# Hybrid attention block, MLP stage: sums of six tile pairs moved to later pairs, weight norms read there, deeper operand preparation in the second product, a row maximum taken earlier

## The chip, the core and the metric

The kernel runs on one core of a Trainium2 chip. The metric is device time in microseconds (us) of one execution of the whole program; lower is better. Engines: PE (matrix products), DVE (VectorE, elementwise work), ACT (ScalarE), POOL (GpSimd), and SP, whose queue issues nearly all DMAs. Each runs its own instructions in order and waits on the others by semaphores. "Pair", "step" and "operand set" below are terms of this kernel.

## What is computed

One transformer layer over 1024 tokens of width 1024, in float32. The change lies in the MLP at its end:

```python
h = rmsnorm(x, g_ff_pre[l])
y = jnp.square(jax.nn.relu(h @ w_ff1[l])) @ w_ff2[l]      # 1024x1024 @ 1024x4096, squared ReLU, @ 4096x1024
x = x + rmsnorm(y, g_ff_post[l])
```

Everything ahead of it (two attention groups, cross-attention to a memory, their projections and norms) is the same code in both kernels.

## The kernel before

Both MLP products use a Strassen-Winograd scheme on 2x2 blocks (seven block products instead of eight), and each float32 product is made of three fast matmuls on a high and a low part: `hi*hi + hi*lo + lo*hi` (lines 195 to 197). In the first product and in most of the second the parts are 16-bit, scaled by powers of two.

**Product one** runs over 16 pairs of hidden-feature blocks (j = 0 to 15). A pair makes the four quadrants of the hidden activation: `g11`, `u3` (the 12 block, later reduced by `pv`), `g22`, `u2`. Seven block products are needed per pair; for j < 7 (`AHEAD`) two of them were made earlier and are read back from DRAM (`reload`, tile `p1r`), so pairs 0 to 6 have 60 matmuls and pairs 7 to 15 have 84. On PE the order within a pair is (h3T products if j >= 7), `px` (T2), `pz` (T1), `px` again (T3, adding to the same bank), `pv` (T4), `pz` again (B22, adding to the same bank). So DVE or ACT must have read `px` before T3 starts, and DVE must have read `pz` (for `g22`) before B22 starts.

After relu and square on ACT (`relu2`, which also leaves a row sum of squares in `hsq`), the pair's quadrants are combined for the second product's Winograd sums. Closure `sums`, called one pair later, makes `s1 = u2 + g22`, `u2 = g11 - u2`, `s2 = s1 - g11`, `s4g = u3 - s2` on DVE (lines 2668 to 2674), stores each to DRAM (`put`, `put_parts`; tensors `gd` and `gi`), and after every odd pair `put_sums` makes four half-width DVE sums for each of two inner blocks and stores them (lines 2200 to 2206).

In the same pair the weights of the next pair are combined: three subtractions and additions and a fourth (lines 2387, 2388, 2389, 2394), on DVE for pairs below 7 and on POOL after that, then split into high (ACT, line 2148) and low parts (DVE, line 2151). Each pair also loads two blocks of `w_ff2` (`norm_load`, tile `w2n`) and squares them on ACT for the weight norm `w2sq` (line 1144), 32 blocks in 16 pairs.

**Product two** has 68 steps, numbered s. Steps 0 to 7 use the T1 sums with 32-bit parts, tile `fy`; later steps use 16-bit parts: 32 steps on full blocks (`fx`) with 28 half-size inner steps (`fi`) between them. For a step, `fetch` loads the left rows `ra` and the right weights (`wg` or `wi`), `combine` makes a weight sum on DVE, `prepare` makes four operand tiles (two ACT, two DVE), `multiply` runs 24 matmuls. Before, three operand sets rotate, `prepare(s + 2)` stands at the head of step s, and `fetch(s + 4)` follows. `second_scales`, at the head of step 3, computes the two scales for the 16-bit steps: PE sums the weight norms (`norms`), DVE takes the row maximum of `hsq` into `scs`, PE transposes that (`top`), DVE and POOL finish. The last three steps run once per output tile, with the final norms and stores (`finish`) between. `later` is a list of such norm work (`squares`, `inverse`, `finish`), from which each step calls one or two entries.

The order of instructions on each engine is that of the code (a manual schedule); tiles come from pools (`u4` has 30 buffers of 4 KB per partition, `wraw` 3, `t2` 18), and a tile waits until its buffer's last user is done.

Of the kernel before, what the change touches and what calls it, by code (L numbers as in the profile page):

```python
# [14 lines left out]
F32 = mybir.dt.float32  # L15
F32R = mybir.dt.float32r
# [121 lines left out]
def build(ctx, tc, nc, out, t):  # L138
# [16 lines left out]
    def u4(name, shape, dt=F32R):  # L155

        return up.tile(list(shape), dt, tag="u4", bufs=30, name=name)
# [2017 lines left out]
    def put(j, i, c):  # L2175
        nc.sync.dma_start(gd[i][j // 2][:, j % 2, :], c)
# [10 lines left out]
    def put_parts(n, j, c):  # L2187

        k, s = j // 2 % 4, j // 8
        if j % 2 == 0:  # L2190
            even[n] = c
            nc.sync.dma_start(gi[n, "A11"][s][:, k, :], c[:, :HQ])
        else:
            nc.sync.dma_start(gi[n, ("A12", "A22")][s][:, :, k, :], c.rearrange("p (a n) -> p a n", a=2))

    def put_sums(n, j, c):

        k, s, e = j // 2 % 4, j // 8, even.pop(n)
        s12, s34 = t2(f"s12_{n}{j}"), t2(f"s34_{n}{j}")
        nc.vector.tensor_add(s12[:, :HQ], e[:, HQ:], c[:, HQ:])  # L2200
        nc.vector.tensor_sub(s12[:, HQ:], s12[:, :HQ], e[:, :HQ])
        nc.vector.tensor_sub(s34[:, :HQ], e[:, :HQ], e[:, HQ:])
        nc.vector.tensor_sub(s34[:, HQ:], c[:, :HQ], s12[:, HQ:])
        return lambda: (
            nc.sync.dma_start(gi[n, ("S1", "S2")][s][:, :, k, :], s12.rearrange("p (a n) -> p a n", a=2)),
            nc.sync.dma_start(gi[n, ("S3", "S4")][s][:, :, k, :], s34.rearrange("p (a n) -> p a n", a=2)))

    def first_row(j, wa, tags=(None, None)):

        x = bank(f"px{j}", tags[0])  # L2210
        product(x, wa, 0, B11)
        yb = bank(f"py{j}", tags[1])
        product(yb, wa, HT, B21)
        p1 = t2(f"p1_{j}")
        nc.scalar.activation(p1, x, AF.Copy)
        g11 = t2(f"g11_{j}")
        return x, p1, g11, lambda: nc.vector.tensor_add(g11, yb, p1)

    was = {}

# [233 lines left out]
    def second_scales():  # L2454

        ps, pt_ = mm_tile([P, 2 * NP], "norms2", "mm"), mm_tile([P, P], "top", "mm")
        nc.tensor.matmul(ps, o1024.to_broadcast([P, P]), w2sq, start=True, stop=True)
        nc.vector.tensor_reduce(su, hsq, axis=mybir.AxisListType.X, op=ALU.max)
        nc.tensor.transpose(pt_, su.to_broadcast([P, P]), ident)
# [90 lines left out]
    def prepare(s):  # L2550

        ra = rows_a.pop(s)
        if s not in right:
            combine(s)
        rb = right.pop(s)
        half = steps[s][0] != 3
        dt = F16 if half else F32R
        if s % 3 == 1 or s == len(steps) - 1:
            ah, al, bh, bl = [u4(f"{m}{s}", (P, D), dt) for m in ("ah", "al", "bh", "bl")]
        else:  # L2560
            ah, al = [wp.tile([P, D], dt, tag=m, bufs=2, name=f"{m}f{s}") for m in ("whi", "wlo")]
            bh, bl = [pws[s % 3 // 2].tile([P, D], dt, tag=f"v{s % 3 // 2}{m}", bufs=1, name=f"v{m}f{s}")
                          for m in ("hi", "lo")]
        if half:
            nc.scalar.activation(ah, ra, AF.Copy, scale=su)  # L2565
            nc.scalar.activation(bh, rb, AF.Copy, scale=sw2)  # L2566
            nc.vector.scalar_tensor_tensor(al, ra, su, ah, op0=ALU.mult, op1=ALU.subtract)  # L2567
            nc.vector.scalar_tensor_tensor(bl, rb, sw2, bh, op0=ALU.mult, op1=ALU.subtract)  # L2568
            ops[s] = (ah, al, bh, bl)
            return  # L2570
        nc.scalar.activation(ah, ra, AF.Copy)
        nc.scalar.activation(bh, rb, AF.Copy)
        nc.vector.tensor_sub(al, ra, f(ah))
        nc.vector.tensor_sub(bl, rb, f(bh))
        ops[s] = (ah, al, bh, bl)

    with manual:
        sums, stores = (lambda: []), []
        for j in range(NP):
# [8 lines left out]
                after.load(0)  # L2588
            elif more:
                fetch(0)  # L2590
            norms = [norm_load(2 * j), norm_load(2 * j + 1)]
            for store in stores:
                store()
            if j < AHEAD:
# [3 lines left out]
                x, _, g11, add = first_row(j, w["a"])  # L2598
                add()
            if not more:  # L2600
                fetch(1)
                fetch(2)
                prepare(0)
            product(x, w["s23"], 0, XT["T2"], more=j >= AHEAD)
            u2 = t2(f"u2_{j}")
            if j < AHEAD:
                nc.vector.tensor_add(u2, x, p1)
            else:
# [14 lines left out]
            u3 = t2(f"u3_{j}")  # L2623
# [4 lines left out]
            g22 = t2(f"g22_{j}")  # L2628
            nc.vector.tensor_add(g22, z, u3)
            stores = [form() for form in forms[:1]]  # L2630
            if late:
# [3 lines left out]
            if after:  # L2635
                after.load(1)
            elif not more:
                prepare(1)
                fetch(3)
            if j + 1 < AHEAD:  # L2640
                reload(j + 1)
            for store in stores:
                store()
            v = bank(f"pv{j}")
            for norm in norms:
                norm()
            product(v, w["s1a"], HT, XT["T4"])
            if more:
                nxt.split("s1a")
# [4 lines left out]
            if more:  # L2654
                nxt.split("s4")
            relu2(u3)
            put_parts(1, j, u3)
            nc.vector.tensor_add(u2, z, u2)
            stores = [form() for form in forms[1:]]
# [4 lines left out]
            def sums(j=j, u2=u2, u3=u3, g11=g11, g22=g22):  # L2664
                if j + 1 < NP:
                    relu2(u2)
                s1, s2, s4g = t2(f"s1_{j}"), t2(f"s2_{j}"), t2(f"s4_{j}")
                nc.vector.tensor_add(s1, u2, g22)
                put(j, 3, s1)
                nc.vector.tensor_sub(u2, g11, u2)  # L2670
                put(j, 5, u2)
                nc.vector.tensor_sub(s2, s1, g11)
# [5 lines left out]
            cur, nxt = nxt, after  # L2678
        prepare(2)


# [142 lines left out]
                finished("i", x)  # L2824

        for s, (n, k) in enumerate(steps[:-3]):
            if s and s < len(steps) - 2:
                prepare(s + 2)
            for read in reads:
                read()  # L2830
            del reads[:]
# [8 lines left out]
            if s + 4 == len(steps):  # L2840
                prepare(s + 3)
# [19 lines left out]
            del later[:1 if n < 6 else 2]  # L2861
# [7 lines left out]
        assert len(later) < 4  # L2869
# [76 lines left out]
```

## Time and profile before

| | |
|---|---|
| median of 3 runs | 1459.2 us (1459.01 to 1463.08) |
| the profiled execution | 1455.45 us, of which its span 1453.7 us |
| PE busy | 97% of the span |
| DVE busy | 78% of the span |
| product one, pairs 1 to 6 | 891.28 to 979.59 us |
| product one, pairs 7 to 14 | 979.59 to 1126.34 us |
| product two | 1144.28 us to the end |

The view of windows gives, for each stretch of the span, its length, each engine's busy time, the clock that PE was granted (1.00 is full), the mean busy share of the 16 DMA engines and the rate they moved. The view of waits lists who waited for whom, with total, count and longest. Timeline rows give start, duration, engine, line and tiles, and in brackets the idle time ahead of an instruction with what ended it. Busy PE is modelled, so stalls are better read from waits and from the start times.

### The profile page before, as it was taken

How to read it: one execution, taken by the hardware profiler on the slowest of the kernel's cores; microseconds unless marked ns; L12 is line 12 of the kernel's file. 1: busy time of each engine (PE TensorE's matmuls, PEld its weight loads, DVE VectorE, ACT ScalarE, POOL GpSimd, SP SyncE). 2: the span in 40 equal slices, each digit the busy share in tenths (PEclk: the TensorE clock that was granted, in tenths of full speed). 3: DMA queues.
4: the chain of work that ended last, by engine and by line, in shares of the span. 5: the costliest groups of instructions: out<-in, count | busy, mean ns of one | idle time of the engine just before them, and what ended most of it. 6: DMA issues, size and time to landing. Idle time of an engine off the chain costs nothing. (4 is left out here: it accounts for less than half of the span.)

```text
span 1453.7 us, 22157 instructions
## 1 busy us (share of the span) xinstructions
PE 1412.0 (97%) x7510; PEld 1019.7 (70%) x7510; DVE 1140.8 (78%) x1940; ACT 964.5 (66%) x1703; POOL 370.7 (26%) x475
## 2 busy tenths in 40 slices
PE   8999999999999999999999999989999979999997
PEld 8988888888889888888888844434444665665653
DVE  6788777866677856779888787887666756899998
ACT  6567887877787835885566566677777626565653
POOL 1245455645454210311113511003332000000003
PEclk9999999999999999999999999999999989999999
DMA  7144547544535585542134638997767987686885
GB/s 277 49 129 117 178 126 254 156 159 139 156 97 152 164 297 196 189 159 88 44 133 172 224 125 284 315 321 263 236 235 250 340 288 252 230 308 231 308 290 206
DMA packets 118801, 295.70 MB, mean 203 GB/s; under 512 B 13448, under 2 KB 31888, under 8 KB 118688
## 3 DMA queue, kind: packets, MB, share of 16 engines
q1 hardware_dynamic: 118544, 294.03, 59.6%
q8 instruction: 59, 0.97, 0.3%
q14 instruction: 54, 0.44, 0.1%
q10 hardware_dynamic: 144, 0.26, 0.1%
HBM read 220.26 MB, written 65.59 MB: 197 GB/s over the span
## 5 line engine op out<-in xcount | busy, mean ns | idle before, releaser
L731 DVE TENSOR_TENSOR phl<-ptr,phl 128x512 fp32r<-128x512 f32 (+1 forms) x152 | 93.3, 616 | 37.7 <-ACT phl L734 36.8
L734 ACT ACTIVATE phl<-ptr 128x512 fp32r<-128x512 f32 (+1 forms) x152 | 81.1, 539 | 35.4 <-PE ptr L725 33.3
L768 PE MATMUL pv<-phl,vs 128*128 128x512 f32 (+1 forms) x304 | 86.4, 367 | 1.8 <-DVE phl L731 1.8
L2565 ACT ACTIVATE whif<-ra,scs 128x1024 f16<-128x1024 f32 x40 | 45.7, 1144 | 41.2 <-PE fx L196 19.7
L2711 POOL TENSOR_SCALAR rf<-sf 128x1 f32<-128x1 f32 x7 | 6.3, 894 | 258.8 <-ACT jf L2690 258.7
L2567 DVE SCALAR_TENSOR_TENSOR wlof<-ra,scs,whif 128x1024 f16<-128x1024 f32 x40 | 51.2, 1281 | 22.6 <-ACT whif L2565 22.6
L196 PE MATMUL fx<-vlof,whif 128*128 128x512 f16 x168 | 63.7, 379 | 1.8 <-DVE vlof L2568 1.8
L195 PE MATMUL fx<-vhif,whif 128*128 128x512 f16 x168 | 63.7, 379 | 0.4 <-ACT vhif L2566 0.4
L197 PE MATMUL fx<-vhif,wlof 128*128 128x512 f16 x168 | 63.7, 379 | 0.0
L768 PEld LDWEIGHTS pv<-phl,vs 128*128 128x128 f32 x304 | 55.0, 188 | 11.6 <-DVE phl L731 2.3
L782 POOL TENSOR_TENSOR o<-o 64x256 f32<-64x256 f32 x64 | 47.5, 742 | 56.8 <-DVE o L780 39.6
L2387 POOL TENSOR_TENSOR sc<-wf,wf 128x512 f32<-128x512 f32 x8 | 12.0, 1506 | 179.9 <-DMA gi1S<-s 96.7
L1606 POOL TENSOR_SCALAR mp<-mp,mst 128x256 f32<-128x256 f32 x32 | 24.6, 774 | 125.1 <-DVE mst L1605 85.8
L195 PE MATMUL k<-hT_hi,whik 128*128 128x512 f32 x128 | 53.2, 415 | 0.0
L195 PE MATMUL q<-hT_hi,whiq 128*128 128x512 f32 x128 | 52.6, 411 | 0.0
L780 DVE TENSOR_TENSOR o<-pv,o 64x512 f32<-64x512 f32 x64 | 43.9, 686 | 10.1 <-ACT o L785 9.1
L195 PE MATMUL yw<-whiwo,yT_hi 128*128 128x512 f32 x128 | 50.7, 396 | 0.0
L197 PE MATMUL q<-hT_hi,wloq 128*128 128x512 f32 x128 | 50.3, 393 | 0.0
L197 PE MATMUL k<-hT_hi,wlok 128*128 128x512 f32 x128 | 50.2, 393 | 0.0
L196 PE MATMUL k<-hT_lo,whik 128*128 128x512 f32 x128 | 50.2, 392 | 0.0
L196 PE MATMUL q<-hT_lo,whiq 128*128 128x512 f32 x128 | 50.1, 392 | 0.0
L196 PE MATMUL yw<-wlowo,yT_hi 128*128 128x512 f32 x128 | 50.1, 392 | 0.0
(818 smaller groups left out, 5129.7 us busy)
## 6 DMA issues: line engine op xcount, KB each, us to landing
wg<-in_w_ff SPq DMA_DIRECT2D x48, 512.0 KB, 5.0
ra<-gd SPq DMA_DIRECT2D x40, 512.0 KB, 4.7
wf<-in_w_ff SPq DMA_DIRECT2D x38, 512.0 KB, 4.2
wn<-in_w_ff SPq DMA_DIRECT2D x32, 512.0 KB, 4.4
w2n<-in_w_ff SPq DMA_DIRECT2D x32, 512.0 KB, 5.8
wi<-in_w_ff2q SPq DMA_DIRECT2D x28, 512.0 KB, 5.1
gd<-s SPq DMA_DIRECT2D x32, 256.0 KB, 3.2
gd<-g SPq DMA_DIRECT2D x25, 256.0 KB, 2.7
```

The lines of the kernel that those rows point to most:

```text
L195: nc.tensor.matmul(ps, lh, rh, start=start, stop=False, skip_group_check=more)
L196: nc.tensor.matmul(ps, lh, rl, start=False, stop=False, skip_group_check=more)
L197: nc.tensor.matmul(ps, ll, rh, start=False, stop=stop, skip_group_check=more)
L731: flow.put("V", at, 0.7, lambda: nc.vector.tensor_sub(pl[:, live, :], tr[:, live, :], f(ph[:, live, :])), done)
L734: flow.put("S", flow.end, 0.6, lambda ph=ph, tr=tr, live=live: nc.scalar.activation(ph[:, live, :], tr[:, live, :], AF.Copy), split)
L768: nc.tensor.matmul(pv[:, :, qs_, :], v, hl[:, :, hs, :], start=c == 0 and turn == 0, stop=last)
L780: flow.put("V", at, 0.7, lambda: nc.vector.tensor_add(o2[own], pv[own, :, :, ::step], o2[own]), lambda end: (free["pv"].give(end), flow.pu ...
L782: free["pv"].give(end), flow.put("G", end, 0.8, lambda: nc.gpsimd.tensor_add(o2[own, 0], o2[own, 0], o2[own, 1]), store)))
L1606: mul = lambda st=st, pr=pr: nc.gpsimd.tensor_scalar(pr, pr, st[:, 2:3], 1.0, op0=ALU.mult, op1=ALU.mult)
L2387: eng.tensor_sub(sc[:, k1], r0[:, k0], r1[:, k0])
L2565: nc.scalar.activation(ah, ra, AF.Copy, scale=su)
L2567: nc.vector.scalar_tensor_tensor(al, ra, su, ah, op0=ALU.mult, op1=ALU.subtract)
```

## The change

It has four parts.

- **Sums put off.** For j < 6, three of the four sums (`u2 = g11 - u2`, `s2`, `s4g`) with their stores, and both `put_sums` of the odd pairs, go into a list, `later_sums`: 6 parts and 6 `put_sums`. Pairs from 7 on call one entry (even j) or two (odd j) at their end; by pair 14 the list is empty. `s2` is now `g22 - u2` of the new `u2`. `u2` and `g22` of these pairs lie in a `u4` tile (`ug`) and `u3` takes the place of `p1` in `p1r`, so that they survive.
- **Weight norms.** Pairs 7 to 14 load four `w2n` blocks each, two squared ahead of the `pv` product and two after `relu2(u3)`; the other pairs load none.
- **Product two.** Four operand sets; steps 0 to 4 still prepare two steps ahead, step 5 prepares 7 and 8, and from there it is three ahead. Steps 0 and 1 are fetched in pair 14, 2 to 5 in pair 15, and then `fetch(s + 5)`. `ra` of the first eight steps lies in `u4`. One entry of `later` is called per step, three at the last.
- **Row maximum.** The reduction of `hsq` stands in step 1, and `second_scales` in step 4.

```diff
+    PUT_OFF = 6
+    later_sums = []
+
+    def put_off_sums(j, u2, u3, g11, g22):
+        r = {}
+        def part():
+            nc.vector.tensor_sub(u2, g11, u2)
+            put(j, 5, u2)
+            s2, s4g = t2(f"s2_{j}"), t2(f"s4_{j}")
+            nc.vector.tensor_sub(s2, g22, u2)
+            put(j, 4, s2)
+            nc.vector.tensor_sub(s4g, u3, s2)
+            put_parts(5, j, s4g)
+            r["s4"] = s4g
+        later_sums.append(part)
+        if j % 2:
+            later_sums.append(lambda: put_sums(1, j, u3)())
+            later_sums.append(lambda: put_sums(5, j, r["s4"])())
...
-        nc.vector.tensor_reduce(su, hsq, axis=mybir.AxisListType.X, op=ALU.max)
         nc.tensor.transpose(pt_, su.to_broadcast([P, P]), ident)
...
-        ra = wp.tile([P, D], F32, tag="wraw", bufs=3, name=f"ra{s}")
+        ra = (u4(f"ra{s}", (P, D), F32) if n == 3 else
+              wp.tile([P, D], F32, tag="wraw", bufs=3, name=f"ra{s}"))
...
-            norms = [norm_load(2 * j), norm_load(2 * j + 1)]
+            norms = [norm_load(4 * (j - AHEAD) + x) for x in range(4)] if AHEAD <= j < AHEAD + NK else []
...
+            put_off = j < PUT_OFF
+            both = u4(f"ug{j}", (P, 2, HT), F32) if put_off else None
+            u2 = both[:, 0, :] if put_off else t2(f"u2_{j}")
...
-            for norm in norms:
+            for norm in norms[:2]:
                 norm()
...
             relu2(u3)
+            for norm in norms[2:]:
+                norm()
...
                 nc.vector.tensor_add(s1, u2, g22)
                 put(j, 3, s1)
+                if j < PUT_OFF:
+                    put_off_sums(j, u2, u3, g11, g22)
+                    return []
...
+            if j >= AHEAD:
+                for call in later_sums[:1 + j % 2]:
+                    call()
+                del later_sums[:1 + j % 2]
...
         for s, (n, k) in enumerate(steps[:-3]):
-            if s and s < len(steps) - 2:
+            if s and s < len(steps) - 2 and s < 5:
                 prepare(s + 2)
+            if s == 5:
+                prepare(7)
+            if 5 <= s:
+                prepare(s + 3)
...
-            if s == 3:
+            if s == 1:
+                nc.vector.tensor_reduce(su, hsq, axis=mybir.AxisListType.X, op=ALU.max)
+            if s == 4:
                 second_scales()
...
-            if s + 4 < len(steps):
-                fetch(s + 4)
+            if s and s + 5 < len(steps):
+                fetch(s + 5)
...
-            for call in later[:1 if n < 6 else 2]:
+            m = 3 if s + 4 == len(steps) else 1
+            for call in later[:m]:
                 call()
```

Every engine has as many instructions after the change as before; they stand in another order. Three places show it. On DVE, in pair 4 from the sum that frees `px` to the one that frees `pz` (`u2_4` from `px4`, then `g22_4` from `pz4`), before:

```order
L2607 TENSOR_TENSOR u2_4_10731<-px4_10718,p1r4_10667 128x512
L2668 TENSOR_TENSOR s1_3_10735<-u2_3_10608,g22_3_10657 128x512
L2670 TENSOR_TENSOR u2_3_10608<-p1r3_10534,u2_3_10608 128x512
L2672 TENSOR_TENSOR s2_3_10736<-s1_3_10735,p1r3_10534 128x512
L2674 TENSOR_TENSOR s4_3_10737<-u3_3_10655,s2_3_10736 128x512
L2387 TENSOR_TENSOR sc5_10762<-wf5_10587,wf21_10665 128x512
L2388 TENSOR_TENSOR wf21_10665<-wf21_10665 128x512
L2389 TENSOR_TENSOR sc5_10762<-wf21_10665,wf5_10587 128x512
L2625 TENSOR_TENSOR u3_4_10778<-px4_10718,p1r4_10667 128x512
```

and after the change (`ug4` holds `u2` and `g22`, `p1r4` takes `u3`):

```order
L2632 TENSOR_TENSOR ug4_10655<-px4_10642,p1r4_10597 128x512
L2696 TENSOR_TENSOR s1_3_10659<-ug3_10548 128x512
L2408 TENSOR_TENSOR sc5_10678<-wf5_10533,wf21_10595 128x512
L2409 TENSOR_TENSOR wf21_10595<-wf21_10595 128x512
L2410 TENSOR_TENSOR sc5_10678<-wf21_10595,wf5_10533 128x512
L2650 TENSOR_TENSOR p1r4_10597<-px4_10642,p1r4_10597 128x512
L2654 TENSOR_TENSOR ug4_10655<-pz4_10665,p1r4_10597 128x512
L2415 TENSOR_TENSOR sd5_10696<-wf5_10533,sc5_10678 128x512
```

Three sums of pair 3 have left the stretch, and four half-width `put_sums` no longer stand between `g22` and `sd`.

On DVE, at the end of pair 10 and the start of pair 11 (`s12_59`, `s34_59` are the `put_sums` of pair 9, `g11_11` the first sum of pair 11, `s1_10` the first sum of pair 10), before:

```order
L2658 TENSOR_TENSOR u2_10_11647<-pz10_11665,u2_10_11647 128x512
L2200 TENSOR_TENSOR s12_59_11755<-s4_8_11499,s4_9_11653 128x256
L2201 TENSOR_TENSOR s12_59_11755<-s12_59_11755,s4_8_11499 128x256
L2202 TENSOR_TENSOR s34_59_11756<-s4_8_11499 128x256
L2203 TENSOR_TENSOR s34_59_11756<-s4_9_11653,s12_59_11755 128x256
L2217 TENSOR_TENSOR g11_11_11803<-py11_11788,p1_11_11801 128x512
L2668 TENSOR_TENSOR s1_10_11821<-u2_10_11647,g22_10_11700 128x512
```

and after the change:

```order
L2686 TENSOR_TENSOR u2_10_11559<-pz10_11577,u2_10_11559 128x512
L2200 TENSOR_TENSOR s12_59_11669<-s4_8_11391,s4_9_11567 128x256
L2201 TENSOR_TENSOR s12_59_11669<-s12_59_11669,s4_8_11391 128x256
L2202 TENSOR_TENSOR s34_59_11670<-s4_8_11391 128x256
L2203 TENSOR_TENSOR s34_59_11670<-s4_9_11567,s12_59_11669 128x256
L2226 TENSOR_TENSOR ug3_10548<-p1r3_10490,ug3_10548 128x512
L2229 TENSOR_TENSOR s2_3_11677<-ug3_10548 128x512
L2231 TENSOR_TENSOR s4_3_11678<-p1r3_10490,s2_3_11677 128x512
L2217 TENSOR_TENSOR g11_11_11729<-py11_11714,p1_11_11727 128x512
L2696 TENSOR_TENSOR s1_10_11747<-u2_10_11559,g22_10_11612 128x512
```

The three sums of pair 3 (`ug3`, `s2_3`, `s4_3`) stand between `put_sums` and `g11_11`, where nothing stood before.

On PE, around `top` in product two, before:

```order
L197 MATMUL fy33_12599<-vhif2_12582,wlof2_12581 128x512
L2457 MATMUL norms2_12738<-w2sq_10215,o1024_81 128x32
L2459 MATMUL top_12739<-ident_72,scs_10216 128x128
L195 MATMUL fy30_12596<-vhif3_12627,whif3_12625 128x512
L196 MATMUL fy30_12596<-vlof3_12628,whif3_12625 128x512
```

and after:

```order
L197 MATMUL fy33_12593<-bh3_12621,al3_12620 128x512
L2478 MATMUL norms2_12770<-w2sq_10215,o1024_81 128x32
L2479 MATMUL top_12771<-ident_72,scs_10216 128x128
L195 MATMUL fy30_12590<-vhif4_12672,whif4_12670 128x512
L196 MATMUL fy30_12590<-vlof4_12673,whif4_12670 128x512
```

`top` stands one step later, ahead of step 4. On DVE the reduction that it waits for stood behind the operands of step 5 and the last `put_sums`, before:

```order
L2539 TENSOR_TENSOR wg1_5_1_12646<-wg1_5_1_12646,wg0_5_1_12648 128x1024
L2573 TENSOR_TENSOR wlof5_12723<-ra5_12644,whif5_12722 128x1024
L2574 TENSOR_TENSOR vlof5_12725<-wg1_5_1_12646,vhif5_12724 128x1024
L2200 TENSOR_TENSOR s12_115_12730<-u3_14_12350,u3_15_12523 128x256
L2201 TENSOR_TENSOR s12_115_12730<-s12_115_12730,u3_14_12350 128x256
L2202 TENSOR_TENSOR s34_115_12731<-u3_14_12350 128x256
L2203 TENSOR_TENSOR s34_115_12731<-u3_15_12523,s12_115_12730 128x256
L2458 TENSOR_REDUCE scs_10216<-hsq_10214 128x1
L2460 TENSOR_REDUCE scs_10216<-norms2_12738 128x1
```

and after the change it stands ahead of the operands of step 4:

```order
L2704 TENSOR_TENSOR s2_15_12630<-s1_15_12627,g11_15_12441 128x512
L2706 TENSOR_TENSOR s4_15_12631<-u3_15_12519,s2_15_12630 128x512
L2878 TENSOR_REDUCE scs_10216<-hsq_10214 128x1
L2560 TENSOR_TENSOR wg1_4_2_12534<-wg1_4_2_12534,wg0_4_2_12536 128x1024
L2595 TENSOR_TENSOR wlof4_12671<-ra4_12532,whif4_12670 128x1024
L2596 TENSOR_TENSOR vlof4_12673<-wg1_4_2_12534,vhif4_12672 128x1024
```

The reduction moved ahead of the operands of steps 4 and 5 and of both `put_sums` of pair 15.

More of the change, by code (lines that the diff above doesn't have):

```diff
@@ L2190, in put_parts @@
         if j % 2 == 0:
-            even[n] = c
+            even[n, j // 2] = c
             nc.sync.dma_start(gi[n, "A11"][s][:, k, :], c[:, :HQ])
@@ L2196, in put_sums @@
     def put_sums(n, j, c):
-        k, s, e = j // 2 % 4, j // 8, even.pop(n)
+        k, s, e = j // 2 % 4, j // 8, even.pop((n, j // 2))
         s12, s34 = t2(f"s12_{n}{j}"), t2(f"s34_{n}{j}")
@@ L2555, in prepare @@
         rb = right.pop(s)
[L2556 to L2564, printed above, removed]
+        if steps[s][0] != 3:
+            q, x = divmod(s % 4, 2)
+            both = [pws[x].tile([P, 2, D], F16, tag=f"v{x}{m}", bufs=1, name=f"v{m}f{s}") for m in ("hi", "lo")] if q else \
+                [wp.tile([P, 2, D], F16, tag=m, bufs=2, name=f"{m}f{s}") for m in ("whi", "wlo")]
+            ah, al, bh, bl = ops[s] = [both[i][:, j] for i in range(2) for j in range(2)]
             nc.scalar.activation(ah, ra, AF.Copy, scale=su)
@@ L2568, in prepare @@
             nc.vector.scalar_tensor_tensor(bl, rb, sw2, bh, op0=ALU.mult, op1=ALU.subtract)
-            ops[s] = (ah, al, bh, bl)
             return
+        if s % 2:
+            ah, al, bh, bl = [u4(f"{m}{s}", (P, D)) for m in ("ah", "al", "bh", "bl")]
+        else:
+            ah, al = [wp.tile([P, D], F32R, tag=m, bufs=2, name=f"{m}f{s}") for m in ("whi", "wlo")]
+            bh, bl = [pws[s % 4 // 2].tile([P, D], F32R, tag=f"v{s % 4 // 2}{m}", bufs=1, name=f"v{m}f{s}")
+                          for m in ("hi", "lo")]
         nc.scalar.activation(ah, ra, AF.Copy)
@@ L2627, in build @@
                 nc.scalar.activation(u3, x, AF.Copy)
-            g22 = t2(f"g22_{j}")
+            g22 = both[:, 1, :] if put_off else t2(f"g22_{j}")
             nc.vector.tensor_add(g22, z, u3)
@@ L2656, in build @@
             relu2(u3)
+            for norm in norms[2:]:
+                norm()
             put_parts(1, j, u3)
@@ L2676, in sums @@
                 return [lambda: put_sums(1, j, u3), lambda: put_sums(5, j, s4g)] if j % 2 else []
+            if j >= AHEAD:
+                for call in later_sums[:1 + j % 2]:
+                    call()
+                del later_sums[:1 + j % 2]
             cur, nxt = nxt, after
+        assert not later_sums
         prepare(2)
@@ L2858, in build @@
             multiply(banks, range(4), [s], n in (2, 4, 6))
-            for call in later[:1 if n < 6 else 2]:
+            m = 3 if s + 4 == len(steps) else 1
+            for call in later[:m]:
                 call()
-            del later[:1 if n < 6 else 2]
+            del later[:m]
             if n == 6 and k in (3, 4):
@@ L2868, in build @@
                 finished(n)
-        assert len(later) < 4
+        assert len(later) <= 4
         last = inverse_last(7)
```

15 lines of the change are left out of this document (7 added, 8 removed).

## The prediction

> **What bounds the kernel now.** I read the view of PE's waits from pair 1 on first, then the windows by stage, then the DVE timeline at each place where PE waits.
>
> ```profile
> PE top L2459 <- DVE scs L2458: 10.5, 1, 10.5
> PE pz L195 <- DVE g L2629: 5.4, 6, 1.9
> PE px L195 <- DVE u L2607: 2.9, 4, 1.0
> PE fx L196 <- DVE vlof L2568: 1.8, 2, 0.9
> PE fx L195 <- ACT bh L2566: 1.1, 1, 1.1
> PE fx L196 <- DVE bl L2568: 0.9, 1, 0.9
> ```
> ```profile
> 891.28:979.59 88.31, 79.80 (x361) 35.01 (x360) 77.06 (x117) 64.29 (x117) 0.00 (x0) 1.00 0.90 307
> 979.59:1126.34 146.75, 146.32 (x673) 65.73 (x672) 102.06 (x131) 104.18 (x188) 45.03 (x32) 1.00 0.72 245
> 997.94:1016.28 18.34, 18.29 (x85) 8.22 (x84) 11.26 (x17) 12.90 (x24) 5.37 (x4) 1.00 0.64 226
> 1144.28:1160.99 16.71, 16.71 (x74) 13.70 (x73) 12.91 (x15) 10.69 (x17) 0.00 (x0) 1.00 0.98 354
> 1160.99:1201.45 40.46, 29.93 (x124) 24.22 (x123) 23.04 (x38) 12.55 (x15) 0.55 (x1) 0.87 0.83 287
> ```
>
> PE is the bound almost everywhere, so time can only come from its stalls, and they lie in three places: pairs 1 to 6 (first window), `top` in step 3 of product two (fifth), and the 16-bit steps late in product two (the three `fx` rows, 3.8 us). Pairs 7 to 14 (second window) have next to none. A change that moves DVE work is worth what it takes from PE in the first place, less what it puts on PE in the second.
>
> **Sums put off, pairs 1 to 6.** Pair 4 on DVE, and the PE instruction that waits for it:
>
> ```profile
> 939.19 0.69 DVE L2607 TENSOR_TENSOR u<-px,p1r 128x512 f32<-128x512 f32 x1 [1.04 <-DMA p1r<-p1d]
> ...
> 941.85 0.69 DVE L2674 TENSOR_TENSOR s<-u,s 128x512 f32<-128x512 f32 x1
> ...
> 945.23 0.69 DVE L2629 TENSOR_TENSOR g<-pz,u 128x512 f32<-128x512 f32 x1
> 945.84 0.41 DVE L2200 TENSOR_TENSOR s<-u,u 128x256 f32<-128x256 f32 x1
> ```
> ```profile
> 945.97 0.38 PE L195 MATMUL pz<-B_hi,u0hi_s 128*128 128x512 f16 x1 [0.69 <-DVE g L2629]
> ```
>
> From `u2` to `g22` DVE works without a pause, so the three sums that leave (lines 2670 to 2674, 3 x 0.69 = 2.07 us) bring `g22` forward by that much, more than the longest of the six waits for it (1.9). `u2` itself waits for `p1r`. Its load is issued behind a weight load which waits for `sd`, and `sd` follows `g22` and, every second pair, four `put_sums` of 0.41; all of that comes 2.07 to 3.7 us sooner, against waits of at most 1.0 by the PE row. The queue also loses two norm loads of 512 KB and some 0.6 MB of stores a pair from a window that is 0.90 full. ACT loses two squares. What is late next is PE alone: 84 matmuls take 18.34 us in the third window, so 60 take 13.1, six pairs 78.6, against 88.31. Gain 9.7 us, between 8.3 (the two PE rows) and 10.7 (if even the last 0.2 us a pair goes).
>
> **The same work in pairs 7 to 14.** DVE gets 6 x 2.07 + 24 x 0.42 = 22.5 us, 2.8 a pair, ahead of `g11`. The end of pair 10 and what follows, on DVE and POOL, and the PE instruction behind:
>
> ```profile
> 1056.12 1.37 DVE L2201 TENSOR_TENSOR s<-s,s 128x256 f32<-128x256 f32 x1
> 1057.41 1.48 DVE L2202 TENSOR_TENSOR s<-s 128x256 f32<-128x256 f32 x1
> 1058.82 0.41 DVE L2203 TENSOR_TENSOR s<-s,s 128x256 f32<-128x256 f32 x1
> ...
> 1062.93 0.69 DVE L2668 TENSOR_TENSOR s<-u,g 128x512 f32<-128x512 f32 x1 [3.10 <-ACT u L2173]
> ...
> 1067.99 0.68 DVE L2629 TENSOR_TENSOR g<-pz,u 128x512 f32<-128x512 f32 x1
> ```
> ```profile
> 1052.51 1.61 POOL L2387 TENSOR_TENSOR sc<-wf,wf 128x512 f32<-128x512 f32 x1 [12.42 <-DMA wf<-in_w_ff]
> ...
> 1057.29 1.33 POOL L2394 TENSOR_TENSOR sd<-wf,sc 128x512 f32<-128x512 f32 x1
> ```
> ```profile
> 1068.72 0.38 PE L195 MATMUL pz<-B_hi,u1hi_s 128*128 128x512 f16 x1
> ```
>
> `g22` ends at 1068.67 and PE takes `pz` at 1068.72: this chain has no slack from `s1` (1062.93) on, but 3.10 us of idle DVE stand before it. In such a pair the deferred part (2.07) runs after POOL's last operation (1058.62) and fits with 1.0 us left. Pairs without `put_sums` here have their time too (3.3 us for the last three rows of them) and take 3.4 to 4.1 us. Under POOL a half-width sum takes up to 1.48 instead of 0.42, so the bounds are 0, if the idle time covers all, and 24 x 1.06 + 18 x 1.06 + 22.5 = 67 us of DVE, less 8 x 3.1 idle, so 42, if every one of the 42 deferred operations is slowed like the worst row. I take 1.2, near the lower end, since POOL works 6.1 of 18.3 us in a pair and the first three slots there are already held by `put_sums` in every second pair.
>
> [...]
>
> ACT has two more squares a pair behind `relu2(u3)`, where it is idle until `px` is done; SP issues two more loads and about three more stores a pair, none ahead of a weight that is due. Bytes are the nearer question:
>
> ```profile
> w2n<-in_w_ff SPq DMA_DIRECT2D x16, 512.0 KB, 5.4
> wf<-in_w_ff SPq DMA_DIRECT2D x15, 512.0 KB, 3.9
> gd<-s SPq DMA_DIRECT2D x16, 256.0 KB, 2.9
> ```
> ```profile
> DMA packets 3355, 8.98 MB, mean 374 GB/s; under 512 B 366, under 2 KB 754, under 8 KB 3353
> ```
>
> The second window takes in 16 norm loads (8.4 MB), the put-off stores (7.4 MB, of 128 to 256 KB) and step 1's loads (1.6 MB): 17.4 MB over 146.75 us, 119 GB/s on top of 245, so 364. The last row is of 1136 to 1160 us, where the queues ran full at 374. So it fits by 3%, and transfers will land later than now.
>
> **Row maximum and `top`.** DVE ahead of the reduction:
>
> ```profile
> 1166.52 1.23 DVE L2539 TENSOR_TENSOR wg<-wg,wg 128x1024 f32<-128x1024 f32 x1 [2.61 <-DMA wg<-in_w_ff]
> ...
> 1171.56 0.21 DVE L2458 TENSOR_REDUCE scs<-hsq 128x1 f32<-128x64 f32 x1
> ```
>
> PE waits 10.5 us for this 0.21 us reduction because step 5's operands, which need step 5's loads, stand ahead of it. In step 1 it needs `relu2` alone, done long before, so `top` in step 4 waits for nothing. The clock of that window, 0.87, comes with the idle time; steps 0 to 2 took 16.71 us, so five take 27.8, against 40.46. Gain 12.6 us, the wait and the slow matmuls behind it; 10.5 if the clock drops anyway.
>
> That holds if steps 3 to 7 then find their operands. DVE has 3.67 us a step (3 x 1.22), and from step 3's operands (done 1156.0 by the same order) to step 7's there are 14.7 of operands, 2.8 of sums, 3.4 of `put_sums` and some 3 of scales: 1180, against step 7's start at 1144.3 + 7 x 5.57 = 1183. ACT needs 2.1 us a step. Loads: steps 2 to 5 are issued in pair 15, and 12.6 MB for all eight steps at 374 GB/s are 34 us, which now begin in pair 14. So nothing is short, by 3 us.
>
> **Four sets, three steps ahead.** The late waits are all for operands of a step just prepared; at the end two steps are prepared in one:
>
> ```profile
> 1432.62 1.28 DVE L2568 SCALAR_TENSOR_TENSOR bl<-wg,scs,bh 128x1024 f16<-128x1024 f32 x1
> 1433.82 4.06 DVE L2735 SCALAR_TENSOR_TENSOR xf<-yc,rf,xf 128x512 f32<-128x512 f32 x6
> ```
>
> DVE is full there, so work is not saved, only done earlier: one more step of lead is 2.6 to 3.8 us (two operations of 1.28 and mostly a combine of 1.22), and four entries of `later` (three of 0.7, one of 1.4) move behind the last operands. That is more than the waits. Gain 3.8 us of waits and about 1.1 of slow clock after them, so 4.9, between 2 (lead not reached) and 6. The moved entries add one `finish` and three `squares` (3.5 us) to a tail in which PE works 15 us; that hides them.
>
> **Sum.** -9.7 + 1.2 - 12.6 - 4.9 = -26.0 us. The profiled execution took 1455.45 us, 0.26% under the median of the runs, so 1429.4 on its footing and 1459.2 - 26.0 = 1433 on the median's, which I predict. A difference of 0.3% is about what a measurement here can tell.
>
> **Rivals.** (1) *Pairs 7 to 14 take much of it back* (0.13). A `wf` load landing later than its 3.9 us starts POOL later, and the deferred sums, which have 1.0 us to spare, run under POOL or behind it, with PE one for one behind. `w2n` at 5.4 shows loads that queue. If `wf` lands 3 us later, six pairs lose 2 us each: 1445. For it: 364 against 374 GB/s. Against: 1067.99 to 1068.72 shows no loss in any pair now. [...]
>
> (2) *The wait at `top` only moves* (0.07). If steps 5 to 7 lack their loads (2.61 us of such a wait stands above), half of the 12.6 returns: 1439. Against: step 5 is now fetched in pair 15.
>
> (3) *Slower* (0.03). [...]
>
> (4) *No change* (0.02): pairs 1 to 6 might be held by DMA (0.90 full) rather than by DVE, `top` by loads, and both waits stay under other names. Against: DVE shows no pause from `u2` to `g22`.
>
> **Numbers.** My forecast, 1425 to 1441, has 0.75. The low end is every stall gone (10.7 + 12.6 + 6) on the profiled footing, 1426, so 1424; the high end takes in rivals 1 and 2, 1446. Faster 0.95, same 0.02, slower 0.03.
>
> **What would show it.** Right: no waits of `pz` on `g` or of `px` on `u` in pairs 1 to 6, these near 79 us; no wait of `top`, and a clock near 1.00 through steps 3 to 7; pairs 7 to 14 at 18.3 to 18.6 us each; no wait over 0.5 us in the last three steps. Wrong: a wait of `pz` on `g` in pairs 8 to 13 with POOL starting more than 1 us into the pair; ACT waiting for `w2n`; DVE waiting for `wg` in steps 4 to 7; or the late `fx` waits unchanged because DVE, not its lead, is what is short.

## The result, and the profile after

The changed kernel takes 1445.95 us (median of 4 runs, 1444.89 to 1447.34), the kernel before 1459.11 (4 runs, 1457.05 to 1463.08): ratio 0.9907, 95% interval 0.9885 to 0.993. It is 13 us faster. 1433 was forecast, and a gain of 26. The time lies above the 1425 to 1441 that had 0.75, and just below 1446, the end that was set for rivals 1 and 2.

Both kernels issue 7510 matmuls, so a stage can be cut at the same matmul in both. The view of windows before (length, then busy time and instructions of PE, PEld, DVE, ACT and POOL, then clock, DMA share, GB/s), for pairs 1 to 6 from the `pz` product of pair 0 on, for pairs 7 to 15, for the steps around step 55 and for the last steps:

```profile
880.05:979.59 99.54, 90.10 (x408) 39.60 (x407) 83.04 (x124) 68.67 (x122) 5.40 (x4) 1.00 0.90 311
979.59:1144.28 164.69, 164.26 (x757) 73.89 (x756) 116.46 (x150) 115.94 (x207) 45.03 (x32) 1.00 0.74 255
1330.21:1350.01 19.80, 18.13 (x110) 10.58 (x109) 19.57 (x22) 10.46 (x10) 0.00 (x0) 1.00 0.56 199
1425.03:1440.21 15.18, 11.86 (x53) 5.08 (x52) 14.99 (x19) 4.89 (x7) 3.41 (x5) 1.00 0.61 201
```

The same matmuls after the change, with steps 3 to 7 as the third row (40.46 us before):

```profile
880.20:968.11 87.91, 87.91 (x408) 39.84 (x407) 64.75 (x88) 54.82 (x97) 5.52 (x4) 1.00 0.61 201
968.11:1152.79 184.68, 168.36 (x757) 74.59 (x756) 135.70 (x186) 131.93 (x236) 44.32 (x32) 0.97 0.87 307
1169.52:1197.23 27.71, 27.71 (x124) 22.64 (x123) 23.06 (x37) 12.60 (x14) 0.55 (x1) 1.00 0.92 346
1325.99:1344.57 18.58, 17.81 (x110) 10.59 (x109) 18.34 (x19) 10.20 (x10) 0.00 (x0) 1.00 0.59 214
1419.59:1430.82 11.23, 11.23 (x54) 5.10 (x53) 10.73 (x16) 4.48 (x11) 7.03 (x10) 1.00 0.42 157
```

| stage | forecast | measured |
|---|---|---|
| pairs 1 to 6 | -9.7 | 87.91 - 99.54 = -11.6 |
| pairs 7 to 15 | +1.2 | 184.68 - 164.69 = +20.0 |
| steps 3 to 7 | -12.6 | 27.71 - 40.46 = -12.8 |
| late product two | -4.9 | (18.58 - 19.80) + (11.23 - 15.18) = -5.2 |
| sum | -26.0 | -9.6 |

Three terms came as forecast and a little better; one missed by 19 us. The forecast's own windows are narrower than two of these. Its pairs 1 to 6 went from 88.31 to 77.70 us, so 10.6 of the 11.6; the other 1.0 is the end of pair 0. Its pairs 7 to 14 went from 146.75 to 159.06, so +12.3; the other 7.7 us are pair 15 (17.94 before, 25.62 after), for which the forecast had no term. (The two spans differ by 1453.7 - 1444.3 = 9.4, the medians by 13.2: the profiled execution before is 3.7 us under its median. Pairs 1 to 6 of the old code are one place that varies: below, two other runs with the same code there take 100.80 and 102.55 us against 99.54.)

All that PE waits for from 880 us on, after the change (total, times, longest):

```profile
PE px L195 <- ACT p L2215: 13.6, 5, 5.9
PE pz L195 <- DVE g L2654: 2.3, 2, 1.2
PE fx L195 <- DVE yc L2800: 0.8, 1, 0.8
```

The waits of pairs 1 to 6 and of `top` are gone. A new one of 13.6 us in all stands in front of T2 in five of the pairs 9 to 15: there PE adds to `px` only once ACT has copied it into `p`. With 2.3 us for `pz` and 168.36 - 164.26 = 4.1 us of slower matmuls that makes the 20.0. The longest case is pair 15, on ACT and then PE:

```profile
1128.91 1.06 ACT L1144 ACTIVATE w2n<-w2n 128x1024 f32<-128x1024 f32 x1 [7.26 <-DMA w2n<-in_w_ff]
...
1137.79 0.57 ACT L2215 ACTIVATE p<-px 128x512 f32<-128x512 f32 x1
```
```profile
1138.42 0.59 PE L195 MATMUL px<-T_hi,v1hi_s 128*128 128x512 f16 x1 [5.90 <-ACT p L2215]
1138.80 0.63 PE L196 MATMUL px<-T_lo,v1hi_s 128*128 128x512 f16 x1
```

ACT stands 7.26 us in front of a norm square of pair 14 whose load has not landed; `p` of pair 15 is queued behind it. Why the load is late is seen on SP's queue, at the turn of pair 10 to 11, before and then after:

```profile
1055.12 0.33 SPq L2192 DMA_DIRECT2D gi1A<-u  x1
1055.54 0.38 SPq L2136 DMA_DIRECT2D wf<-in_w_ff  x1
1055.97 0.92 SPq L2451 DMA_DIRECT2D w2n<-in_w_ff  x2
```
```profile
1048.55 0.33 SPq L2192 DMA_DIRECT2D gi1A<-u  x1
1052.52 0.32 SPq L2176 DMA_DIRECT2D gd<-ug  x1
1054.19 0.32 SPq L2176 DMA_DIRECT2D gd<-s  x1
1055.87 0.53 SPq L2194 DMA_DIRECT2D gi5A<-s  x1
1056.45 0.60 SPq L2136 DMA_DIRECT2D wf<-in_w_ff  x1
1057.10 1.95 SPq L2472 DMA_DIRECT2D w2n<-in_w_ff  x4
```

From the store of the old pair's `u3` (`gi1A`) to the norm loads it was 0.85 us and is now 8.55. Between them stand three stores of put-off sums, and each waits for its DVE sum:

```profile
1050.75 1.75 DVE L2226 TENSOR_TENSOR ug<-p1r,ug 128x512 f32<-128x512 f32 x1
1052.53 1.64 DVE L2229 TENSOR_TENSOR s<-ug 128x512 f32<-128x512 f32 x1
1054.20 1.64 DVE L2231 TENSOR_TENSOR s<-p1r,s 128x512 f32<-128x512 f32 x1
```

### The profile page after: what moved, and what is told of

Read it like the earlier page. It is cut to its first block, busy times and chain, and to the rows that moved or that the text cites. A ratio compares the mean times of both kernels' runs of the same rounds, so it can differ in the third digit from the quotient of the medians.

```text
span 1444.3 us, 22129 instructions
## 1 busy us (share of the span) xinstructions
PE 1409.6 (98%) x7510; PEld 1017.7 (70%) x7510; DVE 1140.6 (79%) x1940; ACT 965.3 (67%) x1703; POOL 369.8 (26%) x475
## 4 chain that ended last, share of the span: by engine, by line
PE 80%; DVE 8%; ACT 4%; DMA 4%; issue 3%; SPq 0%; DVEq 0%; ACTq 0%
PE pv L768 4%; PE ptr L725 4%; PE fx L195 3%; PE fx L197 3%; PE fx L196 3%; DMA w2n<-in_w_ff 2%; PE yw L195 2%; PE k L195 2%; PE q L195 2%; PE yw L197 2%; PE yw L196 2%; PE q L197 2%; PE k L197 2%; PE k L196 2%; PE q L196 2%
## 5 line engine op out<-in xcount | busy, mean ns | idle before, releaser
L734 ACT ACTIVATE phl<-ptr 128x512 fp32r<-128x512 f32 (+1 forms) x152 | 81.1, 540 | 35.0 <-PE ptr L725 32.9
L768 PEld LDWEIGHTS pv<-phl,vs 128*128 128x128 f32 x304 | 54.9, 188 | 11.6 <-DVE phl L731 2.3
L197 PE MATMUL yw<-whiwo,yT_lo 128*128 128x512 f32 x128 | 50.1, 391 | 0.0
L195 PE MATMUL fx<-vlof,vhif 128*128 128x512 f16 x128 | 48.5, 379 | 0.8 <-DVE yc L2800 0.8
L195 PE MATMUL fx<-wlof,whif 128*128 128x512 f16 x128 | 48.5, 379 | 0.0
L196 PE MATMUL fx<-wlof,whif 128*128 128x512 f16 x128 | 48.5, 379 | 0.0
L197 PE MATMUL fx<-wlof,whif 128*128 128x512 f16 x128 | 48.5, 379 | 0.0
```

The lines of the kernel that those rows point to most:

```text
L195: nc.tensor.matmul(ps, lh, rh, start=start, stop=False, skip_group_check=more)
L196: nc.tensor.matmul(ps, lh, rl, start=False, stop=False, skip_group_check=more)
L197: nc.tensor.matmul(ps, ll, rh, start=False, stop=stop, skip_group_check=more)
L734: flow.put("S", flow.end, 0.6, lambda ph=ph, tr=tr, live=live: nc.scalar.activation(ph[:, live, :], tr[:, live, :], AF.Copy), split)
L768: nc.tensor.matmul(pv[:, :, qs_, :], v, hl[:, :, hs, :], start=c == 0 and turn == 0, stop=last)
```

## The experiments

Theory A: the put-off stores stand ahead of the next pair's loads on SP's queue and hold them back (8.55 us at that turn instead of 0.85), the norm loads come late to ACT, and PE waits for what is queued behind them on ACT. Its rivals are B (bytes), C (four squares a pair are too much for ACT) and DVE's sums getting slower beside POOL (0.69 became 1.64 to 1.75 us at that turn). "Pairs 7 to 15" is 164.7 us before and 184.7 after.

### Stores behind the loads

```diff
-            put(j, 5, u2)
...
+            return lambda: (put(j, 5, u2), put(j, 4, s2), put_parts(5, j, s4g))
...
-                for call in later_sums[:1 + j % 2]:
-                    call()
+                stores += [call() for call in later_sums[:1 + j % 2]]
```

> The changed kernel, but the stores of the put-off sums are issued behind the next pair's loads; the DVE work stays where the change put it. Pairs 7 to 15 (first px of pair 7 to first fy) took 164.7 us before and 184.7 us after the change. Theory A (SP's queue: the weight and norm loads stand behind stores that wait for put-off DVE sums, so they are issued some 7 us late): wf is issued 2 to 4 us into a pair again, the wait of px for ACT's p (13.6 us) goes, pairs 7 to 15 take 165 to 167 us, the whole 1426 to 1430. Theory B (bytes: 364 GB/s are too much for that window): loads still land late, pairs 7 to 15 stay above 175, the whole above 1436. Theory C (four squares a pair on ACT, two of them ahead of p, are too many): no change of the 13.6 us.

1431.77 us (4 runs, 1431.08 to 1432.94), ratio to before 0.9819 (0.9792 to 0.9846). Windows, then PE's waits in pairs 7 to 15:

```profile
968.14:1137.82 169.68, 164.43 (x758) 73.91 (x756) 149.05 (x186) 131.40 (x236) 45.49 (x32) 1.00 0.94 330
```
```profile
PE px L195 <- ACT p L2215: 2.7, 1, 2.7
PE pz L195 <- DVE g L2652: 2.3, 5, 0.7
```

No DVE work was moved, only the place of stores on SP, and 15.0 of the 20.0 us went: A. The stage is nearly 3 us above A's 165 to 167. The wait that is left is pair 15's: in pair 14 the four norm loads stand behind `fetch(0)` and `fetch(1)`. Bytes are no less (330 GB/s, DMA 0.94), so B falls as the main cause.

### Norm loads ahead, weights still behind

```diff
-            norms = [norm_load(4 * (j - AHEAD) + x) for x in range(4)] if AHEAD <= j < AHEAD + NK else []
+            norms = ([norm_load(x) for x in range(4)] if j == AHEAD else next_norms) if AHEAD <= j < AHEAD + NK else []
...
+            if AHEAD <= j < AHEAD + NK - 1:
+                next_norms = [norm_load(4 * (j + 1 - AHEAD) + x) for x in range(4)]
             if j >= AHEAD:
                 for call in later_sums[:1 + j % 2]:
```

> The changed kernel, with the four norm loads of a pair issued ahead of the put-off sums of the pair before it; wf stays behind their stores. It tells the two halves of theory A apart. If ACT's wait for late norm loads is what PE sees, the wait of px for p goes and pairs 7 to 15 take 166 to 170 us (the rest are the pz waits, 2.3 us, and the slow sums beside POOL). [...]

1429.2 us (one run). Windows, then PE's waits in pairs 7 to 15:

```profile
968.67:1135.61 166.94, 164.27 (x758) 73.91 (x756) 149.31 (x186) 131.34 (x236) 44.87 (x32) 1.00 0.94 328
```
```profile
PE pz L195 <- DVE g L2654: 2.5, 5, 0.7
```

The wait of `px` for `p` is gone though stores and `wf` loads stand as after the change. So ACT's wait for late norm loads is the half that PE sees. The other half, late `wf` loads and with them slower DVE sums, is not: DVE is busy 149.31 us here against 135.70 after the change, with 186 instructions in both, and the stage is 17.7 us shorter. In pairs 7 to 15 DVE's busy time is 32.9 over before. The prediction counted 22.5 for the work itself, so an estimate of 10.4 is left for slower sums; PE's whole loss in the stage is 2.2 us.

### Norms two a pair again

```diff
-            norms = [norm_load(4 * (j - AHEAD) + x) for x in range(4)] if AHEAD <= j < AHEAD + NK else []
+            norms = [norm_load(2 * j), norm_load(2 * j + 1)]
```

> The changed kernel, but with the norm loads and squares two a pair in all 16 pairs, ahead of pv. Theory A: the two norm loads of pairs 8 to 15 are still issued 10 us into a pair and land at about 16, 2 us after ACT wants them at 14; so ACT waits 2 to 4 us in several pairs, and pairs 7 to 15 take 172 to 182 us. Theory C: px no longer waits for p, pairs 7 to 15 take under 168. Both: pairs 1 to 6 give back at most 1 of the 11.5 us, since DVE and not DMA held them.

1458.52 us (one run). Pairs 1 to 6, then 7 to 15, and what ACT waits for in the latter:

```profile
879.62:972.33 92.71, 88.83 (x409) 39.63 (x408) 64.87 (x86) 67.76 (x119) 5.40 (x4) 1.00 0.80 266
972.33:1164.83 192.50, 173.65 (x757) 75.89 (x756) 147.83 (x187) 118.99 (x210) 45.18 (x32) 0.95 0.72 251
```
```profile
ACT w2n L1144 <- DMA w2n<-in_w_ff: 25.9, 11, 9.7
```

With half the squares and 251 GB/s the stage got longer, beyond what A expected (172 to 182). ACT waits for norm loads for 25.9 us, after the change for 15.9, and PE waits for DVE's `g22` for 10.3 us instead of 2.3. Why two loads a pair are worse than four stays open: the first square of a pair stands in the same place in both. C falls, and B with it. The second expectation failed: pairs 1 to 6 gave back 4.8 us, not 1.

### Only the norms moved

The kernel before, with the change's norm lines alone:

```diff
-            norms = [norm_load(2 * j), norm_load(2 * j + 1)]
+            norms = [norm_load(4 * (j - AHEAD) + x) for x in range(4)] if AHEAD <= j < AHEAD + NK else []
...
-            for norm in norms:
+            for norm in norms[:2]:
                 norm()
...
             relu2(u3)
+            for norm in norms[2:]:
+                norm()
```

> The kernel before, with only the norm loads and squares moved (four a pair in pairs 7 to 14). Theory A: no put-off stores, so loads are issued 3 to 6 us into a pair as before; no wait of ACT for w2n over 1 us, pairs 7 to 15 take 164.7 to 166 us, the whole 1455 to 1459. Theory C: px waits for p in most pairs, pairs 7 to 15 above 172. Theory B: between, up to 168.

1447.03 us (one run). Pairs 1 to 6, then 7 to 15:

```profile
879.62:971.11 91.49, 88.71 (x409) 39.73 (x407) 81.38 (x124) 54.94 (x97) 5.68 (x4) 1.00 0.75 258
971.11:1135.80 164.69, 164.26 (x757) 73.69 (x756) 116.81 (x150) 130.21 (x236) 43.86 (x32) 1.00 0.87 303
```

Four squares a pair cost pairs 7 to 15 nothing: C is out. The stage moved 303 GB/s, nearly the 307 of the changed kernel, and lost nothing by it: B is out too. But the whole was 8 us below what I expected, all of it in pairs 1 to 6. Moving the norms alone gives 8.1 of their 11.6 us, the sums alone 6.8 (the experiment ahead of this one), both together 11.6.

### What the norms cost in pairs 1 to 6

Two edits of the kernel before: the two squares of pairs 0 to 6 behind `relu2(u3)`, and, apart from that, the squares of these pairs over 64 of 1024 columns.

```diff
-            for norm in norms:
-                norm()
+            if j >= AHEAD:
+                for norm in norms:
+                    norm()
...
             relu2(u3)
+            if j < AHEAD:
+                for norm in norms:
+                    norm()
```

> The kernel before, with only the two norm squares of pairs 1 to 6 on ACT moved behind relu2(u3); the loads stay. Moving loads and squares out of these pairs together took 8.0 us from pairs 1 to 6 (from the pz product of pair 0 to the first px of pair 7: 99.5 to 91.5 us). If the squares' place on ACT ahead of the split of s1a, for which DVE waits up to 2.5 us, is the cause: 5 to 8 us go here too. If the loads are (p1r behind w2n in SP's queue, or bytes): under 2 us go.

```diff
-        return lambda: squares_of(w, w2sq[:, n:n + 1])
+        return lambda: squares_of(w[:, :64] if n < 2 * AHEAD else w, w2sq[:, n:n + 1])
```

> The kernel before, with the norm squares of pairs 0 to 6 taken over 64 of 1024 columns (the rest of those norms is left out); the loads stay whole and in place. From the pz product of pair 0 to the first px of pair 7 the kernel before took 99.5 us, and 100.8 and 102.6 with the same code there in two other runs; without loads and squares 91.5. If it was ACT's time for the squares (2 x 1.24 us a pair): 90.5 to 94. If it was the loads (bytes, SP's queue, ACT waiting for them): 97 to 103.

1460.7 and 1455.96 us (one run each). Pairs 1 to 6 of both:

```profile
880.36:983.41 103.05, 92.59 (x409) 40.31 (x408) 83.89 (x125) 67.48 (x121) 5.40 (x4) 0.97 0.87 301
```
```profile
878.42:979.12 100.70, 90.03 (x409) 39.59 (x408) 81.89 (x124) 59.38 (x125) 5.32 (x4) 1.00 0.89 307
```

Neither the squares' place on ACT nor their time is it by itself (with the short squares ACT is busy 59.38 instead of 68.67 us, and nothing is gained). What is left are the loads. Whether by their bytes (share 0.89, and 0.75 without them), by their slots on SP or by ACT's waiting for them stays open; the last is the least likely, since with the squares moved no such wait of ACT is listed in these pairs.

### The row maximum alone

The kernel before, with one line moved out of `second_scales`, which stays in step 3:

```diff
-        nc.vector.tensor_reduce(su, hsq, axis=mybir.AxisListType.X, op=ALU.max)
...
+            if s == 1:
+                nc.vector.tensor_reduce(su, hsq, axis=mybir.AxisListType.X, op=ALU.max)
             if s == 3:
                 second_scales()
```

> The kernel before, with only the row maximum of hsq taken in step 1 instead of in second_scales, which stays in step 3. If the reduction's place in DVE's order is the whole of the wait: the wait of top (10.5 us) goes, the granted clock stays near 1.00, the five steps from fy's first matmul of step 3 on lose 12.6 us, the whole 1445 to 1448. If the later operands were short as well (rival 2 of the prediction): half of it stays as waits of fy in steps 5 to 7. If the clock falls for another reason: 10.5 instead of 12.6.

1448.83 us (one run). Steps 3 to 7, then the last steps:

```profile
1163.58:1192.12 28.54, 28.25 (x124) 22.47 (x122) 21.80 (x37) 12.53 (x15) 0.55 (x1) 1.00 0.98 354
1415.69:1433.59 17.90, 14.80 (x54) 5.70 (x53) 15.04 (x19) 4.89 (x7) 2.76 (x5) 0.81 0.66 219
```

40.46 - 28.54 = 11.9 us came from this one moved instruction, with the clock at 1.00; of the later operands one was waited for, for 0.3 us. The run's other stages gave some of it back, so the whole is just above the 1445 to 1448 expected: its last steps wait about as long as before (3.0 us against 3.3), but the clock was lower, 0.81 against 1.00, and they took 17.90 us against 15.18.

### Late product two

The change there has a lead of three steps, four operand sets with an earlier fetch, and `later` dealt out otherwise. First the changed kernel with the lead of two again:

```diff
-            if s and s < len(steps) - 2 and s < 5:
+            if s and s < len(steps) - 2:
                 prepare(s + 2)
-            if s == 5:
-                prepare(7)
-            if 5 <= s:
-                prepare(s + 3)
+            if s + 4 == len(steps):
+                prepare(s + 3)
```

> The changed kernel, with operands prepared two steps ahead throughout and steps 66 and 67 prepared together, as before; the four operand sets, the loads and the entries of later stay as after the change. If the lead is what removed the late waits of fx: they return, 3 to 5.2 us between step 55 and the end, the whole 1449 to 1451 against 1446. If it was the entries of later (one a step instead of two, three at the end): under 1 us of waits there.

1440.16 us (one run). Around step 55, and the last steps:

```profile
1320.90:1338.67 17.77, 17.77 (x110) 10.67 (x109) 17.61 (x20) 9.45 (x9) 0.00 (x0) 1.00 0.52 182
1413.69:1424.91 11.22, 11.22 (x53) 5.10 (x52) 11.20 (x15) 5.41 (x12) 6.64 (x8) 1.00 0.31 117
```

No wait is left: the lead was not it. (The whole is 5.8 us under the changed kernel's 1445.95; 3.8 of that lie in pairs 7 to 15, which the edit does not touch. That stage varies with the same code: 184.7 us after the change, 180.9 here, 184.1 in the second of the next two runs.) So the two other parts, apart: the kernel before with `later` alone, and the kernel just shown with `later` as before.

```diff
-            for call in later[:1 if n < 6 else 2]:
+            m = 3 if s + 4 == len(steps) else 1
+            for call in later[:m]:
                 call()
...
```

> The kernel before, with only the entries of later dealt as after the change: one a step, three at the fourth step from the end, instead of two in most steps. From step 55 to the end the kernel before loses 5.2 us to waits of fx that the changed kernel does not have. If the entries of later are their cause, they go here: the whole 1450 to 1452 on the footing of 1455.5. If the third operand set was (an operand tile free only when the step before has ended), they stay within 1 us.

> The changed kernel with operands prepared two steps ahead, steps 66 and 67 together, and the entries of later dealt as before (two in most steps); of the changes to product two from step 5 on only the four operand sets and the earlier fetch stay. If the fourth set is what removed the waits of fx, none over 0.5 us come back from step 55 on. If the entries of later are, 3 to 5 us come back. The waits in pairs 7 to 15 stay, since nothing is changed there.

1456.02 and 1446.45 us (one run each). `later` alone, then sets and fetch alone:

```profile
1333.92:1353.72 19.80, 18.14 (x111) 10.59 (x109) 19.57 (x22) 10.46 (x10) 0.00 (x0) 1.00 0.55 198
1428.74:1440.78 12.04, 11.38 (x54) 5.08 (x53) 11.94 (x15) 6.58 (x13) 6.39 (x7) 1.00 0.35 136
```
```profile
1324.43:1342.20 17.77, 17.77 (x111) 10.67 (x110) 17.61 (x20) 9.43 (x9) 0.00 (x0) 1.00 0.52 186
1417.21:1431.21 14.00, 11.71 (x53) 5.08 (x52) 13.87 (x17) 4.89 (x7) 2.38 (x4) 1.00 0.68 219
```

Each does its own part: sets and fetch take all of step 55's 2.0 us and 1.2 of the end's, `later` nothing of step 55's and 3.1 of the end's. Neither expectation was right as a whole. How the sets may work is in ACT's waits from 1250 us on, before, and then after the change:

```profile
ACT whif L2565 <- PE fx L196: 13.1, 7, 2.8
```
```profile
ACT vhif L2582 <- PE fx L197: 6.9, 5, 1.8
ACT whif L2582 <- PE fx L197: 6.2, 4, 2.3
```

With three sets ACT, preparing two steps ahead, waits for PE to finish with the set; in the two kernels with four sets and a lead of two no such wait is listed. With four sets and a lead of three they come back, and step 55 takes 18.58 instead of 17.77. The fourth set was not tried without the earlier fetch, so which of the two did it is not shown.

### Both orders, and the sums dealt out evenly

The changed kernel with the first two edits together; and that with the put-off sums cut into 30 pieces, dealt out by their time over pairs 7 to 14:

```diff
             if j >= AHEAD:
-                for call in later_sums[:1 + j % 2]:
-                    call()
-                del later_sums[:1 + j % 2]
+                due += 6.75
+                while later_sums and later_sums[0][0] <= due:
+                    cost, call = later_sums.pop(0)
+                    due -= cost
+                    stores.append(call())
```

> The changed kernel with two edits: norm loads ahead of the put-off sums, and stores of put-off sums behind the next pair's loads; the put-off sums come in entries as after the change. Theory A: pairs 7 to 15 take 166.5 to 167.5 us, the whole 1426 to 1429; what is left over 164.7 are the waits of pz for g22 in the pairs whose entries are longer than DVE's idle time.

> The changed kernel with three edits: norm loads ahead of the put-off sums, stores of put-off sums behind the next pair's loads, and the put-off sums cut into 30 pieces dealt out evenly, 2.8 us of DVE a pair over pairs 7 to 14. Theory A: pairs 7 to 15 take 165 to 166 us, since no pair's share is over the 3.1 us that DVE was idle; the whole 1425 to 1428. If the slow sums beside POOL matter more than their number, 167 or more.

1429.24 us (4 runs, 1427.97 to 1431.16), ratio 0.9802 (0.9783 to 0.982); and 1427.73 us (5 runs, 1426.98 to 1428.44), ratio 0.979 (0.9773 to 0.9808). Pairs 7 to 15:

```profile
968.59:1134.71 166.12, 164.26 (x757) 73.80 (x756) 143.88 (x186) 131.01 (x236) 46.16 (x32) 1.00 0.94 333
```
```profile
968.61:1134.44 165.83, 164.27 (x758) 73.81 (x756) 142.50 (x186) 131.06 (x236) 46.18 (x32) 1.00 0.94 334
```

Both are faster than the kernel before and than the changed one; between the two the difference is not clear (0.3 us in the stage). The even one came as expected; the other was 0.4 us under its range in the stage and 0.2 us over it in the whole. The even one is at 165.83 against 164.69 before: the work that pairs 1 to 6 gave away then costs 1.1 us.

## Why the prediction was right and where it was wrong

**Pairs 7 to 15, the step that failed.** The prediction said of SP that it issues "two more loads and about three more stores a pair, none ahead of a weight that is due". The stores stand ahead of the next pair's `wf` and `w2n`, and every one waits for a DVE sum. I had counted the put-off part as DVE work and as bytes, and had not followed it down SP's queue. What the step would have shown with the loads in place is in the last experiments: +1.1 us, or +2.2 with the change's own entries and only the norm loads ahead, against the +1.2 taken. So the DVE estimate held. Pair 15, 7.7 of the 20.0 us, was in no term of the sum.

**Rival 1** gave 1445 and a late landing of loads, and 1446 was measured; yet its mechanism was another, so that the time came out inside the range is luck. It had bytes make the loads late (364 against 374 GB/s): the stage moved 307, and 328 to 334 in the four kernels that lost 1 to 5 us there. And it had PE wait for DVE's `g22`: that is 2.3 of 20.0 us. "ACT waiting for `w2n`" stood among the signs of a wrong forecast, without a price. Nor was the stage's mean of 307 the most that was moved there: single slices of it, 4.6 us each, moved up to 412 GB/s.

**Sums beside POOL.** The price of up to 1.06 us for a sum beside POOL is what is seen after the change, at the turn of pair 10 to 11: 0.69 became 1.64 to 1.75, beside POOL operations of 1.30 to 1.60. What makes them slow no run here shows. In the kernel with the norm loads ahead the price comes to an estimated 10.4 us of DVE time in the stage, while PE's whole loss there was 2.2 us, so rival 3, slower, was rightly small.

**Pairs 1 to 6.** The size was nearly right (9.7 against 10.6 in the forecast's own window), the reason half of it. I put all on DVE's three sums and the four `put_sums`, and the norms' departure at nothing. Alone the sums give 6.8 and the norms 8.1, together more than the 11.6 of both: with both, PE is busy for all of its 87.91 us, and there is no wait left to take.

**Row maximum.** As forecast: 12.8 us, the wait of 10.5 and the slow matmuls behind it (before, they start 0.42 to 0.43 us apart from 1172.53 to 1175.94, and 0.23 later on); 11.9 by itself. Rival 2 did not come.

**Late product two.** 5.2 us against 4.9, for a wrong reason: the lead of three steps, to which I gave most of it, adds nothing. The four sets with the earlier fetch, and the entries of `later`, did it. Of the entries the prediction had the right direction ("move behind the last operands").

## What to carry to other kernels

Work that is put off takes its stores along, and where they stand ahead of loads on one queue, the loads wait for the late results too; here, on SP's, the norm loads came 8.55 us behind the old pair's store instead of 0.85, and PE lost 15.0 us to it. Issue the next stage's loads first, and move stores behind them. Follow each queue from the moved instruction to the next load, and from that load to the engine that stands in front of it; here a load for a norm that is not needed until step 4 of product two stopped ACT and so PE. When two parts of a change bear on the same stall, try each alone before giving the gain to one.

## What the runs showed of the hardware

A short wait of PE can cost more than its length, but not each time. In the kernel with the squares moved behind `relu2(u3)`, a wait of 2.18 us was followed by matmuls at half their rate (starts 0.43 us apart instead of 0.21); in the one with stores behind the loads a wait of 2.75 us was not:

```profile
932.87 0.38 PE L195 MATMUL pz<-B_hi,u1hi_s 128*128 128x512 f16 x1 [2.18 <-DVE g L2629]
933.08 0.53 PE L196 MATMUL pz<-B_lo,u1hi_s 128*128 128x512 f16 x1
933.40 0.63 PE L197 MATMUL pz<-B_hi,u1lo_s 128*128 128x512 f16 x1
933.83 0.63 PE L195 MATMUL pz<-B_hi,u1hi_s 128*128 128x512 f16 x1
```
```profile
1125.06 0.38 PE L195 MATMUL px<-T_hi,v1hi_s 128*128 128x512 f16 x1 [2.75 <-ACT p L2215]
1125.27 0.38 PE L196 MATMUL px<-T_lo,v1hi_s 128*128 128x512 f16 x1
```

Other waits went either way. After the change, those of 3.12 and 5.90 us were followed by starts up to 0.43 us apart, and one of 2.31 by starts 0.21 to 0.22 apart, as was one of 2.59 in the kernel with four sets and `later` as before. So 2.18 us were enough once, and 2.75 were not another time; why, no run here shows. The end of product two shows the price: with nearly the same waits (3.3 and 3.0 us) it took 15.18 us in the kernel before and 17.90 with the row maximum alone, at a clock of 1.00 and of 0.81.
